# Rotary embedding on one core: the first batch of x loaded as even partitions, then odd partitions

## The chip, the core and the metric

The kernel runs on one core of a Trainium2 chip. The metric is the time of one execution on the device, in microseconds (us); the median of three runs is used.

## What is computed

```
x:   (16, 512, 1024) float32       # batch, sequence, 16 heads of 64
cos, sin: (512, 32) float32        # one row of 32 for each sequence position
x1, x2 = x[..., :32], x[..., 32:]  # halves of each head
out = concatenate([x1*cos - x2*sin, x1*sin + x2*cos], axis=-1)   # (16, 512, 16, 64) float32
```

Everything stays in float32. x is 33.55 MB and the output is as large, so 67.1 MB have to cross between device memory and the core's on-chip memory.

## The kernel before, in words

**Tiles.** Batches 0, 1, 14 and 15 are tiles of their own ("singles"), the other twelve batches form six pairs: ten tiles, t = 0 to 9. A single puts four sequence positions on each of the 128 partitions, which is one contiguous run of 16 KB of device memory for each partition; a pair puts eight positions on each partition, 32 KB. One sequence position on all 128 partitions is a "row" of 128x1024 numbers (0.5 MB); there are 64 rows, u = 0 to 63. `x_sb` is a ring of 40 rows in on-chip memory, and results are written over the x that they come from.

**Loads.** All are issued by ScalarE's queue (ACTq), in the order of the tiles. The first six tiles (40 rows, 20 MB) fill the ring and are issued at once. After tile 0 the two tables cos and sin (64 KB each) are issued on the same queue (L174), then the other five loads. The remaining four loads wait until the stores that empty their place in the ring have landed (L194).

**Work on a row.** VectorE (DVE) multiplies x by cos into PSUM (`mul`, L293). GpSimd (POOL) multiplies the swapped halves of x by the signed sin table into `t2_sb` (L257); six of the 64 rows have this done by VectorE instead (L286). Then the two are added: for 43 rows by VectorE (`comb`, L304), for 21 rows by TensorE, which adds `t2_sb` into PSUM by a product with the identity (L224), after which ScalarE copies the sum to `x_sb` (L191). GpSimd takes the rows strictly in order.

**Stores.** SyncE's queue (SPq, L161) issues one store for each tile as soon as the last row of the tile is added.

**Start.** A load's completion adds 16 to the tile's semaphore `sem_in[t]`. GpSimd waits at the first row of a tile for that semaphore (L255), and before tile 0 also for the signed sin table, which ScalarE makes from `stage` (L182, L183); VectorE waits for the cos table first (L263), copies it to PSUM (L264), and then waits for the tile's semaphore (L279). TensorE and ScalarE make the tables for the pairs from the same `stage` (L208, L186, L187).

Of the kernel before, what the change touches and what calls it, by code (L numbers as in the profile page):

```python
# [6 lines left out]
def bass_split_heads_rope_kernel(  # L7
# [20 lines left out]
    P = 128  # L28
# [35 lines left out]
    EH = H * HD // BANK  # L64
    LEAD = 1
    LAG = 10

    with ExitStack() as stack:
        x_sb = stack.enter_context(nc.sbuf_tensor([P, RING, H, 2, HALF], fp32))
# [10 lines left out]
        sem_in = [stack.enter_context(nc.semaphore(f"in{t}")) for t in range(NT)]  # L80
# [20 lines left out]
        def c_of(t, r):  # L101
            return c1_ps[:, r, :] if tiles[t][1] == R1 else pair_ps[:, r // R1, 0, r % R1, :]

        def s_of(t, r):
            return s1_sb[:, r] if tiles[t][1] == R1 else s2_sb[:, r]

        x1 = x.rearrange("b (s r) d -> b s (r d)", r=R1)
        o1 = out.rearrange("b (s r) h d -> b s (r h d)", r=R1)
        x2 = x.rearrange("b (s r) d -> s b (r d)", r=R2)
# [3 lines left out]
        def in_dram(single, pairs, t):  # L113
            b, n = tiles[t]
            return single[b] if n == R1 else pairs[:, b:b + 2, :]

        def in_sbuf(t):
            b, n = tiles[t]
            k = b * R1 % RING
            return x_sb[:, k:k + n].rearrange("p n h t d -> p (n h t d)")  # L120

        def where(u):
            t, r = rows[u]
            return t, r, u % RING

        def swapped(k):
            return x_sb[:, k, :, ::-1, :]

        def over_heads(table):
            return table[:, None, :, :].broadcast_to([P, H, 2, HALF])  # L130
# [8 lines left out]
        def wait_t2_free(eng, u):  # L139

            if u >= NT2:
                v = u - NT2
                if PE2[v]:
                    eng.wait_ge(sem_e, n_pe[v])
                else:
                    eng.wait_ge(sem_v, n_comb[v])
# [3 lines left out]
            return sum(b * R1 // R2 == k for b, _ in tiles)  # L150

        def load(eng, t):
            eng.dma_start(in_sbuf(t), in_dram(x1, x2, t)).then_inc(sem_in[t], 16)  # L153

        def on_sync(sp):
            for u in range(NU):
# [7 lines left out]
        def on_scalar(ae):  # L164
            later = {}
            for t, (b, n) in enumerate(tiles):
                if b * R1 + n <= RING:
                    load(ae, t)
                else:

                    later.setdefault((b * R1 - RING) // R2 * R2 + R2 - 1 + LAG, []).append(t)
                if t == 0:
                    for i, (table, sem) in enumerate(((cos, sem_cos), (sin, sem_sin))):
                        ae.dma_start(stage[:, i, :], table.rearrange("(s r) d -> s (r d)", r=R1)).then_inc(sem, 16)  # L174
# [13 lines left out]
            for u in range(NU):  # L188
                if PE2[u]:
                    ae.wait_ge(sem_e, n_pe[u])  # L190
                    ae.activation(xs[:, u % RING, :], t1_ps[:, u % NT1, :], COPY).then_inc(sem_a, 1)  # L191
                for t in later.get(u, ()):
                    k = (tiles[t][0] * R1 - RING) // R2
                    ae.wait_ge(sem_out[k], 16 * stores_of(k))  # L194
                    load(ae, t)
# [38 lines left out]
        def on_gpsimd(pl):  # L234
            pl.memset(ident[:], 1.0).then_inc(sem_i, 1)  # L235
            pl.wait_ge(sem_i, 1)
            pl.affine_select(  # L237
                out=ident[:],
                in_=ident[:],
                compare_op=mybir.AluOpType.is_equal,  # L240
                fill=0.0,
                base=0,
                pattern=[[-1, P]],
                channel_multiplier=1,
            ).then_inc(sem_i, 1)
            for u in range(NU):
                if V2[u]:
                    continue
                t, r, k = where(u)
                if (t, r) == (0, 0):  # L250
                    pl.wait_ge(sem_s, 1)
                if (t, r) == (2, 0):
                    pl.wait_ge(sem_s, 2)
                if r == 0:
                    pl.wait_ge(sem_in[t], 16)  # L255
                wait_t2_free(pl, u)
                pl.tensor_tensor(  # L257
                    t2_sb[:, u % NT2, :, :, :], swapped(k), over_heads(s_of(t, r)), mult
                ).then_inc(sem_p, 1)

        def on_vector(ve):
            ve.memset(zero[:], 0.0).then_inc(sem_z, 1)  # L262
            ve.wait_ge(sem_cos, 16)  # L263
            ve.tensor_copy(c1_ps, stage[:, 0, :].rearrange("s (r d) -> s r d", d=HALF)).then_inc(sem_c, 1)  # L264
            ve.wait_ge(sem_c, 1)
            ve.wait_ge(sem_w, NT1 * EH)

            def pair_tables():
                ve.wait_ge(sem_s, 2)
                row = pair_ps[:, V_ROW // R1, 1, V_ROW % R1, :]  # L270
                ve.tensor_scalar_mul(v_ps[:, 0, :], row, -1.0).then_inc(sem_c, 1)
                ve.tensor_copy(v_ps[:, 1, :], row).then_inc(sem_c, 1)

            first_v = V2.index(True)

            def mul(u):
                t, r, k = where(u)
                if r == 0:
                    ve.wait_ge(sem_in[t], 16)  # L279
                if (t, r) == (2, 0):  # L280
                    pair_tables()
                if u == first_v:
                    ve.wait_ge(sem_c, 3)
                if V2[u]:
                    wait_t2_free(ve, u)
                    ve.tensor_tensor(t2_sb[:, u % NT2, :, :, :], swapped(k), over_heads(v_ps), mult)  # L286
                if u >= NT1:
                    v = u - NT1
                    if PE2[v]:
                        ve.wait_ge(sem_a, n_pe[v])  # L290
                    else:
                        ve.wait_ge(sem_v, n_comb[v])
                ve.tensor_tensor(  # L293
                    t1_ps[:, u % NT1, :].rearrange("p (h d) -> p h d", d=HALF),
                    x_sb[:, k, :, :, :].rearrange("p h t d -> p (h t) d"),
                    c_of(t, r)[:, None, :].broadcast_to([P, 2 * H, HALF]),
                    mult,
                ).then_inc(sem_m, 1)

            def comb(u):  # L300
                t, r, k = where(u)
                ve.wait_ge(sem_m, u + 1)
                ve.wait_ge(sem_p, n_pool[u])  # L303
                ve.tensor_tensor(  # L304
                    xs[:, k, :],
                    t1_ps[:, u % NT1, :],
                    t2_sb[:, u % NT2, :, :, :].rearrange("p h t d -> p (h t d)"),
                    add,
                ).then_inc(sem_v, 1)

            for u in range(NU + LEAD):
                if u < NU:
                    mul(u)
                if u >= LEAD and not PE2[u - LEAD]:
                    comb(u - LEAD)

        on_sync(nc.sync)
        on_scalar(nc.scalar)
        on_gpsimd(nc.gpsimd)
        on_tensor(nc.tensor)  # L320
        on_vector(nc.vector)
# [33 lines left out]
```

## Time and profile before

| | |
|---|---|
| Median of three runs | 161.4 us (161.15 to 161.4) |
| The profiled execution, first to last instruction (its span) | 160.3 us; no time of its own is listed beside it |
| Bytes moved | 67.26 MB, 419 GB/s over the span |
| Share of the span in which an engine is busy | GpSimd 84%, VectorE 81%, TensorE 45%, ScalarE 15% |
| DMA: share of 16 engines' span | loads' queue 49.6%, stores' queue 48.9% |
| Loads: time from issue to landing | 8.0 us shortest, 67.5 us longest |

The page cuts the span into 40 slices of 4.0 us and gives for each the busy share of every engine in tenths. A "landing" is the moment at which a transfer's semaphore has its full count. The time from issue to landing contains the time that a transfer spends behind others in its queue. DMA shares over 1 occur in short stretches because a packet's time is counted by its recorded start and end.

### The profile page before, as it was taken

The page shows a single profiled execution, that of the slowest core. Times are in us where ns is not written, and L with a number is a line of the kernel's source. Part 1 is how long each engine was busy: PE and PEld are TensorE (multiplying, and loading weights), DVE is VectorE, ACT ScalarE, POOL GpSimd, SP SyncE. Part 2 cuts the span into 40 slices and gives each one's busy share as a digit, 9 for nine tenths or more (in the row PEclk, how much of TensorE's full clock was granted, in tenths as well). Part 3 has the DMA queues.
Part 4 walks back from the last instruction along what each step waited for, and adds up shares of the span by engine and source line. Part 5 has one row for each costly group of instructions (what it writes and reads, how often), then busy time and mean ns, then how long its engine had stood idle before and what let it go on. Part 6 is the DMA issues. An engine that isn't in the chain of part 4 may idle for free.

```text
span 160.3 us, 522 instructions
## 1 busy us (share of the span) xinstructions
PE 72.8 (45%) x94; PEld 24.0 (15%) x94; DVE 130.3 (81%) x117; ACT 24.4 (15%) x27; POOL 134.9 (84%) x64
## 2 busy tenths in 40 slices
PE   6050004478357936660847105489458435850000
PEld 1020002022202211210221002022202111220000
DVE  0069998599989999996999709899889999999500
ACT  0420000203120222022012010201220402040000
POOL 1059999999999999999999999699999999289400
PEclk9955555557755587689687965555555977699555
DMA  5999999999999999999999999999999999999896
GB/s 147 409 441 474 409 450 409 425 429 429 446 429 458 417 411 466 409 433 401 450 433 425 425 409 458 409 433 433 411 429 462 441 417 401 450 441 441 376 450 294
DMA packets 3170, 67.26 MB, mean 419 GB/s; under 512 B 352, under 2 KB 608, under 8 KB 608
## 3 DMA queue, kind: packets, MB, share of 16 engines
q10 hardware_dynamic: 1728, 33.69, 49.6%
q1 hardware_dynamic: 1440, 33.56, 48.9%
q14 instruction: 2, 0.02, 0.0%
HBM read 33.69 MB, written 33.55 MB: 419 GB/s over the span
## 4 chain that ended last, share of the span: by engine, by line
DMA 60%; POOL 13%; DVE 8%; PE 7%; issue 3%; ACT 2%; ACTq 1%; DVEq 0%
DMA x_sb<-in_x_dram 41%; DMA out_dram<-x_sb 18%; POOL t_sb L257 13%; PE t_ps L224 7%; DVE t_ps L293 5%; DVE x_sb L304 3%; ACT x_sb L191 2%; ACTq L153 1%; ACTq L174 1%; DVE t_sb L286 0%; DVEq L303 0%
## 5 line engine op out<-in xcount | busy, mean ns | idle before, releaser
L257 POOL TENSOR_TENSOR t_sb<-x_sb,s_sb 128x1024 f32<-128x1024 f32 x58 | 134.2, 2346 | 14.8 <-ACT s_sb L183 8.5
L224 PE MATMUL t_ps<-t_sb,ident 128*128 128x512 f32 x84 | 68.0, 957 | 63.0 <-DVE t_ps L293 39.2
L293 DVE TENSOR_TENSOR t_ps<-x_sb,pair_ps 128x1024 f32<-128x1024 f32 x48 | 57.7, 1223 | 9.9 <-ACT x_sb L191 9.8
L304 DVE TENSOR_TENSOR x_sb<-t_ps,t_sb 128x1024 f32<-128x1024 f32 x43 | 52.4, 1218 | 2.6 <-POOL t_sb L257 2.6
L224 PEld LDWEIGHTS t_ps<-t_sb,ident 128*128 128x128 f32 x84 | 22.1, 290 | 108.9 <-DVE t_ps L293 74.6
L191 ACT ACTIVATE x_sb<-t_ps 128x1024 f32<-128x1024 f32 x21 | 21.5, 1023 | 109.9 <-PE t_ps L224 96.9
L293 DVE TENSOR_TENSOR t_ps<-x_sb,tab_ps 128x1024 f32<-128x1024 f32 x16 | 19.3, 1222 | 0.1
L286 DVE TENSOR_TENSOR t_sb<-x_sb,tab_ps 128x1024 f32<-128x1024 f32 x6 | 7.3, 1213 | 0.0
L264 DVE COPY tab_ps<-stage 128x128 f32<-128x128 f32 x1 | 0.3, 294 | 7.8 <-DMA stage<-in_cos_dram 7.8
L208 PE MATMUL pair_ps<-stage,pick 128*128 128x256 f32 x4 | 2.0, 667 | 5.4 <-DMA stage<-in_sin_dram 5.4
L201 PE MATMUL t_ps<-zero 128*128 128x512 bf16 x6 | 2.7, 627 | 1.3 <-DVE zero L262 1.3
L208 PEld LDWEIGHTS pair_ps<-stage,pick 128*128 128x128 f32 x4 | 1.2, 324 | 6.4 <-issue 6.3
L177 ACT ACT_TABLE_LOAD x1 | 1.3, 1283 | 5.5 <-issue 5.5
L201 PEld LDWEIGHTS t_ps<-zero 128*128 128x128 bf16 x6 | 0.7, 136 | 2.4 <-DVE zero L262 1.2
L262 DVE MEMSET zero<- 128x256 uint32 x1 | 0.3, 272 | 0.9 <-PEq L337 0.9
L186 ACT ACTIVATE s_sb<-pair_ps 128x256 f32<-128x256 f32 x1 | 0.4, 383 | 1.7 <-PE pair_ps L208 1.7
L182 ACT ACTIVATE s_sb<-stage 128x128 f32<-128x128 f32 x1 | 0.3, 309 | 2.1 <-DMA stage<-in_sin_dram 2.1
L235 POOL MEMSET ident<- 128x128 f32 x1 | 0.2, 204 | 0.3 <-POOLq L337 0.3
L177 ACT ACTIVATE pick<-ident 128x256 f32<-128x256 f32 x1 | 0.4, 416 | 0.0
L187 ACT ACTIVATE s_sb<-pair_ps 128x256 f32<-128x256 f32 x1 | 0.4, 379 | 0.0
L237 POOL TENSOR_SCALAR_AFFINE_SELECT ident<-ident 128x128 f32<-128x128 f32 x1 | 0.3, 292 | 0.1
L337 POOL MEMSET const-float32-0.0<- 128x1 f32 x1 | 0.1, 98 | 0.3 <-issue 0.3
(6 smaller groups left out, 1.0 us busy)
## 6 DMA issues: line engine op xcount, KB each, us to landing
x_sb<-in_x_dram ACTq DMA_DIRECT2D x6, 4096.0 KB, 38.0
out_dram<-x_sb SPq DMA_DIRECT2D x6, 4096.0 KB, 25.0
x_sb<-in_x_dram ACTq DMA_DIRECT2D x4, 2048.0 KB, 22.6
out_dram<-x_sb SPq DMA_DIRECT2D x4, 2048.0 KB, 15.2
stage<-in_cos_dram ACTq DMA_DIRECT2D x1, 64.0 KB, 7.8
stage<-in_sin_dram ACTq DMA_DIRECT2D x1, 64.0 KB, 7.5
```

The lines of the kernel that those rows point to most:

```text
L153: eng.dma_start(in_sbuf(t), in_dram(x1, x2, t)).then_inc(sem_in[t], 16)
L174: ae.dma_start(stage[:, i, :], table.rearrange("(s r) d -> s (r d)", r=R1)).then_inc(sem, 16)
L177: ae.activation(pick[:], ident[:].rearrange("q (s k) -> q k s", k=2)[:, :, :, None].broadcast_to([P, 2, P // 2, 2]), COPY).then_inc(sem_g, 1)
L186: ae.activation(s2[:, :, :, 0, :], pair_ps[:, :, 1, :, :], COPY, scale=-1.0)
L191: ae.activation(xs[:, u % RING, :], t1_ps[:, u % NT1, :], COPY).then_inc(sem_a, 1)
L201: pe.matmul(t1_ps[:, k, b * BANK:(b + 1) * BANK], zero[:, 0:P], zero[:], start=True, stop=True).then_inc(sem_w, 1)
L208: pe.matmul(pair_ps[:, k].rearrange("p c r d -> p (c r d)"), pick[:, k].rearrange("q s b -> q (s b)"), stage[:].rearrange("q c f -> q (c f)"),
L224: ins = pe.matmul(t1_ps[:, u % NT1, b * BANK:(b + 1) * BANK], ident[:], t2[:, b * BANK:(b + 1) * BANK], start=False, stop=True, skip_group ...
L257: pl.tensor_tensor(t2_sb[:, u % NT2, :, :, :], swapped(k), over_heads(s_of(t, r)), mult).then_inc(sem_p, 1)
L286: ve.tensor_tensor(t2_sb[:, u % NT2, :, :, :], swapped(k), over_heads(v_ps), mult)
L293: ve.tensor_tensor(t1_ps[:, u % NT1, :].rearrange("p (h d) -> p h d", d=HALF), x_sb[:, k, :, :, :].rearrange("p h t d -> p (h t) d"), c_of ...
L304: ve.tensor_tensor(xs[:, k, :], t1_ps[:, u % NT1, :], t2_sb[:, u % NT2, :, :, :].rearrange("p h t d -> p (h t d)"), add,).then_inc(sem_v, 1)
```

## The change

The load of tile 0 is issued as two transfers, in place of one: first the partitions 0, 2, 4, ..., 126 and then 1, 3, 5, ..., 127, each partition with the same 16 KB as before. Each of the two adds 16 to `sem_in[0]`, so the two waits for tile 0 (on GpSimd and on VectorE) wait for 32. Nothing starts work on one half alone. The tables and all other loads follow behind the two on the same queue, unchanged.

```
+    FIRST = 2
...
         def load(eng, t):
-            eng.dma_start(in_sbuf(t), in_dram(x1, x2, t)).then_inc(sem_in[t], 16)
+            if t:
+                eng.dma_start(in_sbuf(t), in_dram(x1, x2, t)).then_inc(sem_in[t], 16)
+                return
+            for i in range(FIRST):
+                eng.dma_start(in_sbuf(t)[i:P:FIRST], in_dram(x1, x2, t)[i:P:FIRST]).then_inc(sem_in[t], 16)
...
                 if r == 0:
-                    pl.wait_ge(sem_in[t], 16)
+                    pl.wait_ge(sem_in[t], 16 * (FIRST if t == 0 else 1))
...
                 if r == 0:
-                    ve.wait_ge(sem_in[t], 16)
+                    ve.wait_ge(sem_in[t], 16 * (FIRST if t == 0 else 1))
```

## The prediction

> **What bounds the kernel now.** I read the page first, for the shares and the slices.
>
> ```profile
> DMA  5999999999999999999999999999999999999896
> GB/s 147 409 441 474 409 450 409 425 429 429 446 429 458 417 411 466 409 433 401 450 433 425 425 409 458 409 433 433 411 429 462 441 417 401 450 441 441 376 450 294
> q10 hardware_dynamic: 1728, 33.69, 49.6%
> q1 hardware_dynamic: 1440, 33.56, 48.9%
> ```
>
> Only the first slice and the last few are below 9 tenths, and between the first slice and the last the rate stays at 376 to 474 GB/s whether loads run alone (slices 2 to 5), with stores, or stores alone near the end. A rate that doesn't depend on the direction or the mix looks like a ceiling of the 16 DMA engines or of their way into on-chip memory. So DMA time lost anywhere before the last load is lost to the whole stream of loads. The chain that ended last says the same:
>
> ```profile
> 2.87 18.56 DMA x_sb<-in_x_dram
> ...
> 93.45 47.51 DMA x_sb<-in_x_dram
> 140.96 0.07 issue
> 141.02 9.29 POOL t_sb L257 x4
> ...
> 150.40 1.23 DVE x_sb L304
> ```
>
> The last load is issued at 93.4 and lands at 140.96, 47.5 us later, because it stands behind other loads and shares the engines with stores. Behind it come four rows on GpSimd (9.3 us), one addition (1.2) and the last store (issued at 151.7, 8.6 us to the end at 160.3): a tail of 19.3 us that the change doesn't touch. GpSimd's timeline shows the slack ahead of that tail:
>
> ```profile
> 9.85 90.09 POOL L257 TENSOR_TENSOR t_sb<-x_sb,s_sb 128x1024 f32<-128x1024 f32 x39 [8.48 <-ACT s_sb L183]
> 101.72 9.29 POOL L257 TENSOR_TENSOR t_sb<-x_sb,s_sb 128x1024 f32<-128x1024 f32 x4 [1.78 <-PE t_ps L224]
> ...
> 141.02 9.27 POOL L257 TENSOR_TENSOR t_sb<-x_sb,s_sb 128x1024 f32<-128x1024 f32 x4 [3.92 <-DMA x_sb<-in_x_dram]
> ```
>
> The brackets give the idle time before each piece and what ended it. GpSimd is 3.92 us early for the last tile: a late start of the arithmetic alone, with the loads as they are, can be swallowed there; lost DMA time can't.
>
> The start, from the timeline and from the table of short stretches (last three columns: granted clock, DMA share, GB/s):
>
> ```profile
> 0.81 0.37 ACTq L153 DMA_DIRECT2D x_sb<-in_x_dram  x1
> 1.21 0.46 ACTq L174 DMA_DIRECT2D stage<-in_cos_dram  x1
> 1.69 0.45 ACTq L174 DMA_DIRECT2D stage<-in_sin_dram  x1
> ...
> 9.04 0.29 DVE L264 COPY tab_ps<-stage 128x128 f32<-128x128 f32 x1 [7.84 <-DMA stage<-in_cos_dram]
> ```
>
> ```profile
> 1.00:2.00 1.00, 0.75 (x2) 0.28 (x3) 0.19 (x1) 0.00 (x0) 0.29 (x1) 1.00 0.54 98
> 2.00:3.00 1.00, 1.00 (x4) 0.36 (x3) 0.00 (x0) 0.00 (x0) 0.00 (x0) 1.00 0.75 180
> 3.00:4.00 1.00, 0.99 (x3) 0.08 (x1) 0.00 (x0) 0.00 (x0) 0.00 (x0) 1.00 0.83 311
> 4.00:5.00 1.00, 0.00 (x0) 0.00 (x0) 0.00 (x0) 0.00 (x0) 0.00 (x0) 1.00 1.00 426
> ```
>
> Tile 0 is issued at 0.81 and lands 8.0 us later (the shortest time to landing of any load), at 8.8; cos at 9.0, sin at 9.2 (7.8 and 7.5 us after their issue). VectorE waits for cos, GpSimd for sin, which stands last in that queue. The rate climbs for three microseconds: 98 + 180 + 311 GB/s makes 0.59 MB by 4.0.
>
> **The change part by part.** *One more issue on ACTq.* One issue takes 0.37 to 0.46 us with 0.03 between, so cos, sin and the five loads behind them are issued about 0.4 us later. The engines need the tables only when tile 0 is through, near 7.5 (0.59 MB by 4.0, the other 1.51 MB at 426 GB/s: 3.5 us). cos and sin issued at 1.6 and 2.1 are there by then; ScalarE's own first work has 2.08 us of idle time before sin. Cost nothing; without that cover it would be 0.4.
>
> *Sixteen more completion packets.* The loads' queue has 1728 packets for twelve transfers, which is 12 x (128 + 16): one per partition and one per engine for completion. Now it has 1744. The queue's share, 49.6% of 16 x 160.3 us over 1728 packets, is 0.74 us a packet, and those are 19.5 KB on average; a completion packet carries almost nothing. At worst one per engine costs 0.74 us, at best nothing. I take nothing, as the tables' small packets are the nearest: cos and sin, 288 packets together, put only 0.4 us between the landing of tile 0 and that of sin.
>
> *A second landing.* Both waits are now for the second half's landing. Three transfers in one queue land within 0.4 us here, so waiting for completion isn't paid one after the other: cost 0. [...]
>
> *The rate of a transfer to every second partition.* This is the term that decides, and no row here shows one: every transfer in the trace covers 128 partitions. [...] Bounds: at best the half runs at the 426 GB/s of the row at 4.0, cost 0, or the slow climb before 4.0 gets shorter: at 426 from 2.0 on, 0.85 MB would have come in place of 0.49, a gain of at most 0.36 MB / 426 GB/s = 0.85 us. At worst it stays at the lowest rate of a full microsecond with the queue already filled, 180 GB/s: 1.51 MB / 180 in place of 1.51 / 426, 8.4 - 3.5 = +4.9 us. I take half the steady rate, 213 GB/s, that is, that the partitions of one half bring two engines at a time onto one way into on-chip memory. That lies nearer to the 180 row than to the 426 row, and I choose it because the steady rate looks like a ceiling of such ways: it is alike for both directions. 1.51 / 213 = 7.1 in place of 3.5, **+3.5 us**; the climb, which is below or near 213 anyway, is left as it is.
>
> [...]
>
> *Where the loss goes.* The landing of tile 0, the tables, and every later load move by 3.5 us; GpSimd starts at 13.4 in place of 9.85, and everything it paces, the stores included, moves along. Nothing absorbs it: the 3.92 us stay, since the load they wait for is late by as much. Sum: span 160.3 + 3.5 = 163.8. The median of the runs is 1.1 above the span; 161.4 + 3.5 = **164.9 us**.
>
> **The rivals.** *No change.* The halves run at 426 GB/s; the queue hides the rest, 161.4 within 0.3. For it: all partitions get the same bytes in packets of the same 16 KB, and the queue is never empty. Against it: the steady ceiling says that which way an engine uses matters, and the new shape alters that.
>
> *Faster.* Smaller transfers let all engines begin sooner or spread the first reads better, and the climb gains half of its 0.85 us: 161.0. For it: the shares of 0.54, 0.75 and 0.83 before 4.0 show engines without work, or slow, while the queue has it. Against: the first issue comes at the same 0.81. It decides from about 0.7 MB moved by 4.0.
>
> *Slower by latency.* The second half's completion comes 1 to 2 us late though the engines lose nothing, and the slack isn't there when needed (at 101.72 GpSimd waits 1.78 for TensorE, at 141.02 3.92 for the load): up to 162.5. It needs a slip beyond the slack.
>
> **How the numbers follow.** A measurement of this kernel can tell about 0.2% (0.3 us) from no change. Half rate: 0.56, all slower, between 163 and 166.3 (+1.6 for a partial loss, +4.9). No change: 0.22, of which 0.11 within 0.2%, 0.05 below and 0.06 above. Faster start: 0.17. Latency: 0.05. Faster 0.05 + 0.17 = 0.22; same 0.11; slower 0.56 + 0.06 + 0.05 = 0.67. The cases have both signs. The likeliest one's own range is 163.0 to 166.3; the range that is to hold 8 in 10 has to reach to no change and to most of the faster start: 160.9 to 166.3, which leaves out gains over 0.5 us and the odd case above.
>
> **What would show it.** Right: in the stretches from 4.0 to 8.0 the GB/s fall to about 210 to 260 in place of 344 to 442; the cos wait of VectorE ends near 12.5 in place of 9.04; GpSimd's first multiplication starts near 13.4; the second and third slices together carry some 1.5 MB less; the wait at the last tile is still near 3.9 and the tail 19.3. Wrong: 400 GB/s or more from 4.0 on and cos within 0.3 us of 9.0 (no change); or more than 0.7 MB by 4.0 and an earlier cos (faster start). If tile 0 lands late and the end doesn't move, the chain from the first load to the last is what I have misread.

## The result, and the profile after

The changed kernel takes 161.94 us (median of 21 runs) against 161.32 us before (21 runs beside them): a ratio of 1.0037, 95% interval 1.0027 to 1.0046, that is 0.6 us slower (0.4 to 0.7). Ratios and intervals, here and below, are taken from the executions that were not in a slower state of the chip. The forecast was 164.9, 3.5 us slower. The sign was right; the size was wrong by a factor of six.

The page of the changed kernel comes first: the slices, the rates and the loads' queue.

```profile
span 160.2 us, 523 instructions
...
DMA  4999999999999999999999999999999999999896
GB/s 147 391 444 491 393 393 401 450 421 491 397 393 458 419 491 401 401 507 401 393 507 409 393 491 417 401 442 413 440 421 479 405 417 434 454 417 474 356 454 286
...
q10 hardware_dynamic: 1744, 33.69, 49.6%
```

The 16 more packets are there (1744), and the forecast hole in the second and third slices is not: 391 and 444 GB/s, against 409 and 441 before. The span is even 0.1 us shorter than on the page before. That comparison misleads. The span that the runs list for each execution is 1.4 us below its time, in every kernel of this study; the page before has 160.3, but the executions of the same kernel beside the experiments have median spans of 159.8 to 159.9, and the changed kernel's is 160.5. So the page before shows an execution about 0.5 us longer than usual, the page after one of the shortest of its kernel, and a change of 0.6 us can't be read off two pages.

The start of the changed kernel, from its timeline and from the table of short stretches:

```profile
0.81 1.20 ACTq L159 DMA_DIRECT2D x_sb<-in_x_dram  x2
...
2.05 0.60 ACTq L180 DMA_DIRECT2D stage<-in_cos_dram  x1
...
8.86 0.29 DVE L270 COPY tab_ps<-stage 128x128 f32<-128x128 f32 x1 [7.67 <-DMA stage<-in_cos_dram]
```

```profile
1.00:2.00 1.00, 0.75 (x2) 0.28 (x3) 0.20 (x1) 0.00 (x0) 0.29 (x2) 1.00 0.00 0
2.00:3.00 1.00, 1.00 (x4) 0.37 (x3) 0.00 (x0) 0.00 (x0) 0.00 (x0) 1.00 1.09 262
3.00:4.00 1.00, 0.99 (x3) 0.09 (x1) 0.00 (x0) 0.00 (x0) 0.00 (x0) 1.00 0.84 328
4.00:5.00 1.00, 0.00 (x0) 0.00 (x0) 0.00 (x0) 0.00 (x0) 0.00 (x0) 1.00 0.89 377
```

Two things differ from before. The first issue takes 0.56 us where it took 0.37 (the chain lists 0.56 and 0.61 for the two), and no packet starts between 1.0 and 2.0: the trace's first packet of x starts at 2.18 in place of 1.82. These stretches count a packet, with all its bytes and its whole time, where it starts; that is also why shares over 1 occur. So the 0.59 MB (262 + 328) by 4.0, the same as before, are packets begun; of those of x, 0.33 MB had ended by then on either page. From 4.0 to 8.0 the halves run at 391 GB/s, against 406 in the kernel before:

```profile
4.00:8.00 4.00, 0.00 (x0) 0.00 (x0) 0.00 (x0) 1.28 (x1) 0.00 (x0) 1.00 0.94 391
```

```profile
4.00:8.00 4.00, 0.00 (x0) 0.00 (x0) 0.00 (x0) 1.70 (x2) 0.00 (x0) 0.96 0.97 406
```

The first line is of the changed kernel, the second of the kernel before. The tail is as before: the last tile's wait and the four rows after it on GpSimd,

```profile
140.89 9.27 POOL L263 TENSOR_TENSOR t_sb<-x_sb,s_sb 128x1024 f32<-128x1024 f32 x4 [3.83 <-DMA x_sb<-in_x_dram]
```

and 19.3 us from there to the end. Two kernels that turned out as fast as the one before ("second" and "gap" below) have pages with spans of 159.7 and 159.8, the same 19.3 us at the end, and this line at 140.37 and 140.52. So what the change costs arises ahead of the landing of the last load.

### The profile page after: what moved, and what is told of

Same layout as the page of the kernel before. It is cut to its first block, busy times and chain, and to the rows that moved or that the text cites. A ratio compares the mean times of both kernels' runs of the same rounds, so it can differ in the third digit from the quotient of the medians.

```text
span 160.2 us, 523 instructions
## 1 busy us (share of the span) xinstructions
PE 71.3 (44%) x94; PEld 23.8 (15%) x94; DVE 130.4 (81%) x117; ACT 24.4 (15%) x27; POOL 134.8 (84%) x64
## 3 DMA queue, kind: packets, MB, share of 16 engines
q10 hardware_dynamic: 1744, 33.69, 49.6%
## 4 chain that ended last, share of the span: by engine, by line
DMA 59%; POOL 13%; DVE 8%; PE 7%; issue 4%; ACTq 2%; ACT 2%; DVEq 0%
DMA x_sb<-in_x_dram 40%; DMA out_dram<-x_sb 18%; POOL t_sb L263 13%; PE t_ps L230 7%; DVE t_ps L299 5%; DVE x_sb L310 3%; ACT x_sb L197 2%; ACTq L180 1%; ACTq L159 1%; ACTq L156 1%; DVE t_sb L292 0%; DVEq L309 0%
## 5 line engine op out<-in xcount | busy, mean ns | idle before, releaser
L230 PE MATMUL t_ps<-t_sb,ident 128*128 128x512 f32 x84 | 66.5, 937 | 64.3 <-DVE t_ps L299 40.3
L299 DVE TENSOR_TENSOR t_ps<-x_sb,tab_ps 128x1024 f32<-128x1024 f32 x16 | 19.3, 1222 | 0.1
```

Source lines behind the costliest of these rows:

```text
L230: ins = pe.matmul(t1_ps[:, u % NT1, b * BANK:(b + 1) * BANK], ident[:], t2[:, b * BANK:(b + 1) * BANK], start=False, stop=True, skip_group ...
L299: ve.tensor_tensor(t1_ps[:, u % NT1, :].rearrange("p (h d) -> p h d", d=HALF), x_sb[:, k, :, :, :].rearrange("p h t d -> p (h t) d"), c_of ...
```

## The experiments

Each ratio is to the kernel before, timed on the same chip in the same rounds; a loss in us is the ratio less 1, times 161.3. The runs weigh four theories: the prediction's (a transfer to half the partitions runs at half the rate); the first descriptor (a transfer of 64 partitions starts later); something in the second transfer itself; an instruction more, outside the span.

**halves: neighbouring partitions.**

```
-                eng.dma_start(in_sbuf(t)[i:P:FIRST], in_dram(x1, x2, t)[i:P:FIRST]).then_inc(sem_in[t], 16)
+                eng.dma_start(in_sbuf(t)[i * P // FIRST:(i + 1) * P // FIRST], in_dram(x1, x2, t)[i * P // FIRST:(i + 1) * P // FIRST]).then_inc(sem_in[t], 16)
```

> Tile 0 in two transfers as after the change, but partitions 0 to 63 and then 64 to 127. Theory of the first descriptor (a transfer of 64 rows starts its first packets about 0.36 us later, near 2.18 in place of 1.82, and the whole stream of loads is late by some tenths): the same late start and 161.8 to 162.1 us. Theory of the prediction (the partitions of a transfer share ways into on-chip memory, which every second partition happened to escape): neighbouring halves run at half rate, VectorE's wait for cos ends near 12 and the time is 164 to 165. Theory of the instruction outside the span (one more DMA costs a few tenths between the span and the measured time): 161.8 to 162.0, with time minus span near 1.45 us.

Measured: 1.0302 (1.0264 to 1.0341), 4.9 us slower (4.3 to 5.5), above the 164 to 165 us that were expected. Two stretches of 4 us of this kernel (last column GB/s), then its first row on GpSimd:

```profile
4.00:8.00 4.00, 0.00 (x0) 0.00 (x0) 0.00 (x0) 1.70 (x2) 0.00 (x0) 1.00 0.94 197
8.00:12.00 4.00, 0.00 (x0) 0.00 (x0) 0.00 (x0) 0.00 (x0) 0.00 (x0) 1.00 0.97 199
```

```profile
14.43 90.10 POOL L263 TENSOR_TENSOR t_sb<-x_sb,s_sb 128x1024 f32<-128x1024 f32 x39 [13.06 <-ACT s_sb L189]
```

From 4.0 to 8.0 the engines are as busy as in the changed kernel (0.94), yet they move half: 197 GB/s against 391. In the trace a packet of 16 KB that starts in that stretch takes 1.16 to 1.29 us here; in the changed kernel all but a few take 0.61 to 0.64. So a half-rate transfer exists and costs what the prediction reckoned and more; but neighbours have it, not alternate partitions. This settles the main miss. It doesn't say what the neighbours share: they are neighbours in device memory too, where each half is one contiguous 1 MB in place of every second 16 KB, and no run changes one side alone.

**four: four transfers of every fourth partition.**

```
-    FIRST = 2
+    FIRST = 4
```

> Tile 0 in four transfers of every fourth partition. If each further transfer costs (an issue of about 0.6 us each on ScalarE's queue, a bubble at each completion packet): three times the loss of the change, 162.9 to 163.3 us. If only the later first packet costs: 161.8 to 162.1 again, first packets near 2.2. If the instruction outside the span costs: three times 0.35 us between span and time, 162.4 to 162.6 with an unchanged span.

Measured: 1.0102 (1.0056 to 1.0148), 1.6 us slower, with a wide scatter between runs. The interval, 0.9 to 2.4 us, lies above what a late first packet alone would cost (it starts at 2.20; "delay" below prices that) and holds three times the change, 1.9 us; so this run leaves a cost per transfer possible. Time less span stays at 1.4, so nothing is lost outside the span. The stretch from 4.0 to 8.0 has 344 GB/s; its 84 packets of 16 KB take 0.75 us in the mean (busy share 0.99), 25 of them over 0.7 and up to 1.85 us. Why those are slow I didn't find out.

**second: tile 1 split like this, tile 0 whole.**

```
-            if t:
+            if t != 1:
...
-pl.wait_ge(sem_in[t], 16 * (FIRST if t == 0 else 1))
+pl.wait_ge(sem_in[t], 16 * (FIRST if t == 1 else 1))     # and the same on VectorE
```

> Tile 0 whole again, tile 1 in two transfers of every second partition: the same number of instructions and packets as after the change, but the extra one stands behind others in the queue. Theory of the first descriptor: the first packets start at 1.82 again and the time is that of before, 161.2 to 161.5 us. Theory of a bubble at a completion packet or of an extra instruction outside the span: the time of after, 161.8 to 162.1.

Measured: 0.9997 (0.9982 to 1.0011), no difference (at most 0.2 us). Its timeline:

```profile
0.81 0.37 ACTq L156 DMA_DIRECT2D x_sb<-in_x_dram  x1
...
2.18 1.30 ACTq L159 DMA_DIRECT2D x_sb<-in_x_dram  x2
```

The first issue takes 0.37 again and the first packet starts at 1.83. The very same two transfers, with their packets, completions and doubled wait, cost nothing that can be measured when they stand behind others. A cost per completion or per instruction wherever it stands is refuted; the loss belongs to the head of the queue.

**actop: one more instruction, no DMA.**

```
+            ae.activation(spare[:, 0:1], ident[:, 0:1], COPY)
             ae.wait_ge(sem_sin, 16)
```

> The kernel before with one more small copy on ScalarE (128x1), in the idle time before the sin table, and no further DMA. Theory of the first descriptor and theory of a bubble: 161.2 to 161.5 us, as before. Theory that any further instruction costs outside the span: 161.6 to 161.9 with time minus span over 1.3 us.

Measured: 1.0007 (0.9988 to 1.0025), time less span 1.4 again. The interval alone reaches a loss of 0.4 us; it is the unchanged 1.4, here and in the changed kernel, that refutes the theory outside the span.

**delay: tile 0 whole, issued later.**

```
             later = {}
+            ae.wait_ge(sem_z, 1)
```

> The kernel before, tile 0 in one transfer, but ScalarE's queue first waits for VectorE's memset (over at about 1.2 us), so the first issue stands at about 1.23 in place of 0.81. It shows what a late first issue by itself is worth. Theory of the first descriptor: the first packets start at about 2.24, as after the change, and the end moves by as much, 0.4 us: 161.6 to 161.8. Theory that the two transfers cost something in themselves at the head of an empty queue, the late start being hidden in the 3.6 to 3.9 us of slack ahead of the last tile: 161.2 to 161.4.

Measured: 1.0016 (1.0005 to 1.0027), 0.26 us slower (0.08 to 0.44). Its first issue and its last tile:

```profile
1.23 0.37 ACTq L153 DMA_DIRECT2D x_sb<-in_x_dram  x1
...
140.82 9.28 POOL L258 TENSOR_TENSOR t_sb<-x_sb,s_sb 128x1024 f32<-128x1024 f32 x4 [3.59 <-DMA x_sb<-in_x_dram]
```

The first packet starts at 2.25, 0.43 later than before. A late first packet costs, and the wait for the last tile is still 3.6, as in "second" and "gap" (3.58 and 3.62): that slack doesn't swallow it, since the load it waits for is late as well, as far as single pages tell (140.82 here, 140.37 and 140.52 there). By the middle value it accounts for less than half of the change's 0.6; the interval allows anything from 0.1 to 0.4 us of it.

**cols: two transfers of tile 0, all partitions, half of the columns each.**

```
+    W = R1 * dim // FIRST
...
-                eng.dma_start(in_sbuf(t)[i:P:FIRST], in_dram(x1, x2, t)[i:P:FIRST]).then_inc(sem_in[t], 16)
+                eng.dma_start(in_sbuf(t)[:, i * W:(i + 1) * W], in_dram(x1, x2, t)[:, i * W:(i + 1) * W]).then_inc(sem_in[t], 16)
```

> Tile 0 in two transfers that each cover all 128 partitions, with half of every row (8 KB). Theory that a transfer to 64 partitions is issued more slowly: the first issue takes 0.37 again, the first packets start at 1.82 and the time is 161.2 to 161.5 us. Theory that a second issue or a second completion at the head costs: 161.8 to 162.1 as after the change. Theory of packets of half the size: a little above before, within 0.3 us, with 256 packets more in the table of queues than packets of completion.

Measured: 1.0024 (1.0013 to 1.0036), 0.4 us slower (0.2 to 0.6). Its short stretches:

```profile
1.00:2.00 1.00, 0.75 (x2) 0.28 (x3) 0.20 (x1) 0.00 (x0) 0.30 (x2) 1.00 0.35 57
2.00:3.00 1.00, 1.00 (x4) 0.36 (x3) 0.00 (x0) 0.00 (x0) 0.00 (x0) 1.00 0.70 197
3.00:4.00 1.00, 1.00 (x3) 0.09 (x1) 0.00 (x0) 0.00 (x0) 0.00 (x0) 1.00 0.98 377
```

The issues are short again (0.38 and 0.46), the first packet starts at 1.84, and by 4.0 this kernel has begun 0.63 MB, more than before. So the late start does belong to transfers of 64 partitions; yet this kernel loses time without it. Its loss lies between the theories and is not decided: it can come from tile 0 in two transfers, or from its 8 KB packets, for which up to 0.3 us was expected and which the change doesn't have.

**second_halves: tile 1 in neighbouring halves.**

```
-            if t:
+            if t != 1:
...
-                eng.dma_start(in_sbuf(t)[i:P:FIRST], in_dram(x1, x2, t)[i:P:FIRST]).then_inc(sem_in[t], 16)
+                eng.dma_start(in_sbuf(t)[i * P // FIRST:(i + 1) * P // FIRST], in_dram(x1, x2, t)[i * P // FIRST:(i + 1) * P // FIRST]).then_inc(sem_in[t], 16)
...                                                                    # and the waits as in "second"
```

> Tile 1, not tile 0, in two transfers of partitions 0 to 63 and 64 to 127. Theory that neighbouring halves lose their time by half rate wherever they stand in the queue: the loss of the neighbouring halves of tile 0 (4.7 us) less what belongs to the late first packet (0.4 to 0.7), 165.2 to 165.7 us. Theory that half rate costs only while nothing else is in the queue (other transfers behind it fill the gaps): 161.3 to 162.5.

Measured: 1.0389 (1.0373 to 1.0404), 6.3 us slower. The slices of its page show the hole, third and fourth:

```profile
GB/s 166 419 208 233 371 402 410 418 438 442 442 426 454 434 444 394 473 402 465 410 458 426 394 473 410 465 402 467 406 454 418 418 454 414 458 418 402 422 264 316
```

208 and 233 GB/s with 16.8 MB (four pairs) queued behind: the work behind doesn't fill the gaps. Here as in "halves" half rate goes with the shape, not with the start. Both expectations were too low; why this place costs some 1.4 us more than the head is not explained.

**two_queues: the odd partitions issued by SyncE.**

```
-            for i in range(FIRST):
-                eng.dma_start(...)
+            for i, q in enumerate((eng, nc.sync)):
+                q.dma_start(...)
...
+        on_scalar(nc.scalar)                 # so that SyncE's load stands ahead of its stores
         on_sync(nc.sync)
-        on_scalar(nc.scalar)
```

> The two transfers of the change, the even partitions issued by ScalarE's queue and the odd ones by SyncE's queue at about the same time. Theory of the first descriptor: a 64-partition transfer still stands first on both queues, first packets near 2.2, 161.7 to 162.1 us. Theory that it is the second issue, 0.6 us, in front of the tables and the later loads that costs: 161.2 to 161.5.

Measured: 1.0036 (1.0024 to 1.0049), 0.6 us, the same as the change. Each queue issues one:

```profile
0.80 0.58 SPq L159 DMA_DIRECT2D x_sb<-in_x_dram  x1
0.81 0.57 ACTq L159 DMA_DIRECT2D x_sb<-in_x_dram  x1
```

Both take 0.57 to 0.58, and the first packet starts at 2.17. cos is issued at 1.41, only 0.2 later than before, and the whole loss is still there: the second issue in front of the tables isn't what costs, and two issues side by side are no remedy.

**gap: tile 0 whole at 0.81, everything behind it issued later.**

```
                 if t == 0:
+                    ae.wait_ge(sem_w, 2)
```

> The kernel before, tile 0 in one transfer at 0.81, but ScalarE's queue waits after it until TensorE's second product is done (about 2.3 us), so the tables and the later loads are issued about 1.0 us later, as they are behind the second transfer of the change (there 0.84 later). Theory that the place which the second issue takes in the queue is the other part of the cost: 161.6 to 161.8. Theory that the engines still have tile 0 to move until 7.5 and nothing behind it is late: 161.2 to 161.4, and the other part lies in the two transfers themselves.

Measured: 1.0002 (0.9993 to 1.0011), nothing. cos was issued at 2.32 in place of 1.21:

```profile
0.81 0.37 ACTq L153 DMA_DIRECT2D x_sb<-in_x_dram  x1
2.32 0.33 ACTq L175 DMA_DIRECT2D stage<-in_cos_dram  x1
```

The place that the second issue takes on ScalarE's queue is free (at most 0.2 us), as the prediction had it.

**delay_gap: both waits.**

```
             later = {}
+            ae.wait_ge(sem_z, 1)
...
                 if t == 0:
+                    ae.wait_ge(sem_w, 2)
```

> Both waits: tile 0 in one transfer is issued at 1.23 in place of 0.81 and the tables at about 2.3, so all issue times are near those of the change, without its split. Theory that the change costs through issue times alone: 161.8 to 162.0, as after the change. Theory that only the late first packet counts among them: 161.5 to 161.7, as with the first wait alone.

Measured: 161.77 us against 161.29 beside it, 0.5 us by the medians; but the ratio of 1.0009 has an interval, 0.9978 to 1.0039, that includes no loss. Two runs of the kernel before, at 163.27 and 163.56, lie about 2 us above the others in these rounds, while all twelve of this one lie from 161.56 to 161.94. This is inconclusive between the two theories: it doesn't exclude that issue times alone, without the split, make up most of the change's loss.

**tabs_whole and tabs_split: the tables ahead of tile 0, which is whole or split.**

```
-                if b*R1 + n <= RING: load(ae, t)
                 if t == 0:
                     for i, (table, sem) in ...: ae.dma_start(stage[:, i, :], ...)
+                if b*R1 + n <= RING: load(ae, t)
```

> The kernel before with the two tables issued ahead of tile 0, not behind it. It is the base for the next run. The tables' packets take less than a microsecond, tile 0 is issued near 1.7 and its first packets start near 2.7: late by 0.9, which by the rate of the first wait (0.26 us for 0.42) gives 161.6 to 162.0 us.

> The same with tile 0 in the two transfers of the change, so that a transfer of 64 partitions no longer stands first in the queue. Theory that the change costs as the first transfer of an empty queue, and by its slower issue: the engines wait for x at this place too, so a loss of 0.2 to 0.4 us against the run with the tables ahead of the whole tile. Theory that only the very first transfer of the program starts slowly: within 0.2 us of that run. Theory that the second transfer costs at the head in any case: 0.4 to 0.6 us above it.

Measured: 1.0052 (1.0042 to 1.0063) and 1.0066 (1.0057 to 1.0074). "tabs_split" is the same edit, made to the changed kernel. With the tables first, tile 0's first packets start at 2.82 when it is whole and at 3.03 when it is split, and the times are 162.05 and 162.34 us. So the slower start of a 64-partition transfer isn't the program's first issue alone: here it is 0.2 us, and the end is 0.3 us later. That is what the first theory expected, and less than the 0.4 to 0.6 of the theory that the second transfer costs at the head in any case, though the two intervals overlap. Both kernels are slower than before: x should stand first.

**extra, cols_delay, after_again.** The first adds a small transfer between tile 0 and the tables; the second puts the wait of "delay" ahead of "cols"; the third is the changed kernel again.

```
                 if t == 0:
+                    ae.dma_start(spare[:], cos...).then_inc(sem_x, 16)      # extra
...
             later = {}
+            ae.wait_ge(sem_z, 1)                                          # cols_delay, on top of cols
```

> The kernel before, tile 0 in one transfer, with one more small transfer (the cos table a second time, 64 KB, into memory that nothing reads) between tile 0 and the tables. Theory that a second transfer at the head of the queue costs 0.35 us by itself: 161.6 to 161.8. Theory that it has to be a second part of tile 0: its 64 KB at 426 GB/s, 0.15 us, so 161.3 to 161.5.

> Tile 0 in two transfers of half the columns and all 128 partitions, the first of them issued at 1.23 in place of 0.81 by the wait for VectorE's memset. Theory that the late first packet (0.26 us for 0.42) and the second transfer of tile 0 (0.37 us) are two costs that add up to the change: 161.8 to 162.05. Theory that they share one cause: 161.6 to 161.75.

> The changed kernel once more, on the chip and beside the runs of the other two, so that they are compared on equal terms: 161.8 to 162.1 us by both theories.

Measured: 1.0014 (1.0002 to 1.0027), 1.0053 (1.0033 to 1.0074) and 1.0049 (1.0025 to 1.0073). The extra transfer costs 0.2 us (0.0 to 0.4): the middle is near the 0.15 of its own bytes, but the interval holds the 0.35 of the other theory as well, so this run doesn't decide. The late start and the column split together cost 0.5 to 1.2 us, with 0.85 in the middle; their separate losses make 0.26 + 0.39 = 0.65, and the change beside them lost 0.4 to 1.2. So these two add up, and one cause for both (161.6 to 161.75 expected, 162.05 measured) does not fit. The sum also fits the change within what these runs can tell, which doesn't show that the change consists of the same two.

## Why the prediction was right or wrong

**The step that failed** is the rate of a transfer to every second partition. I took half the steady rate, 213 GB/s and +3.5 us, for a shape that no row showed, by arguing that alternate partitions bring two engines onto one way into on-chip memory. That was an assumption: no run shows such a way, nor 213 GB/s for this shape. The runs show that a half rate exists, at 197 to 199 GB/s, for partitions 0 to 63 and 64 to 127, and that alternate partitions escape it: 391 GB/s from 4.0 to 8.0, against 406 before. By the prediction's own sum, an estimate, 1.51 MB at 391 in place of 406 make 0.1 us in place of 3.5. For neighbouring halves the price would have been too low rather than too high: 4.9 us against 3.5. What the argument lacked was the question which partitions go into one transfer. Whether the neighbours share something on the side of on-chip memory or of device memory, no run here shows.

**The rival "no change"** had the rate right and came nearest, but its time of 161.4 within 0.3 misses the measured median by 0.2. The rival "faster" asked for 0.7 MB by 4.0; it was 0.59, as before. What stood against it held: the first issue came at the same 0.81, and it even took longer. The rival "slower by latency" had a mechanism that the runs don't show: no completion came 1 to 2 us late, a figure that no row had given (VectorE's wait for cos ended at 8.86; in "second" and "gap" it was 8.65 and 8.90), and the doubled wait cost nothing in "second".

**The further issue at nothing**: right for the place that it takes in the queue, by "gap"; that an issue would take 0.37 to 0.46 us was wrong for 64 partitions (0.56 and 0.61). **The completion packets and the second landing at nothing**: right where the two transfers stand behind others, by "second"; at the head no run prices them alone. **The slack of 3.9 us ahead of the last tile**: I said that a late start of the arithmetic alone could be swallowed and lost DMA time could not. "delay" agrees with the second half, and it is why a late first packet is seen at the end at all. **The 1.1 us between span and median**: the median time lies 1.4 above the median span; the page before shows a longer execution than most. The sum stands on the median, so nothing came of it.

**What was missing from the sum** is a late start. A transfer of 64 partitions takes 0.56 us to issue in place of 0.37, and its first packet starts 0.36 us later; a wait that makes the first packet 0.43 later costs 0.26 us (0.08 to 0.44). By the middle values that leaves about 0.35 us of the 0.6 to something else.

**What stays open** is that rest. It is not the place of the second issue in the queue ("gap", "two_queues") and not the two transfers wherever they stand ("second"). A second cost of tile 0 in two transfers is the likeliest reading: "cols" loses 0.4 us (0.2 to 0.6) without any late start, and "cols_delay" shows that such a loss and a late start add up. But it isn't shown, since "cols" also doubles the packets, at half the size. Against it, splitting tile 0 behind the tables cost only 0.3 us with a start 0.2 later, and "delay_gap", which has late issues and no split, lost 0.5 us by the medians. Nor does "extra" exclude that any second transfer at the head costs. On the page of "cols" the last load lands at 140.7 though more bytes had been begun by 4.0 than before; single pages scatter by as much as the rest itself, so they can't say where it goes. What was not run is the change's own two transfers at the head without the late start.

**The range**, 160.9 to 166.3, holds the measured time because it reached to "no change", not because the forecast was near. That the sign was right is luck: the loss that was foreseen isn't there, and the one that is there was priced at nothing.

No run of this study beat the kernel before beyond its interval; the whole tile in one transfer, issued first, remains the best start.

## What to carry to other kernels

When a transfer is cut by partitions, ask which partitions go into one transfer before pricing it: here alternate partitions kept 391 GB/s and neighbours fell to 197, in the same number of transfers and bytes. The same cut by alternate partitions cost nothing measurable (at most 0.2 us) behind a filled queue and 0.6 us at the head of an empty one, so look at where in the queue an edit stands before counting its instructions. And before comparing two pages, compare their spans with the spans of the other executions: the page of the slower kernel here was the shorter one.

## What the runs showed of the hardware that was not expected

- Issuing a transfer of 64 partitions as the first took 0.55 to 0.58 us (the change, "halves", "two_queues"), on ScalarE's and on SyncE's queue, against 0.37 to 0.38 for one of 128 partitions; the first packet started at 2.16 to 2.23 against 1.82 to 1.84, where the issue stood at 0.8.
- Transfers to 64 neighbouring partitions keep the engines as busy (share 0.94) at half the rate (197 GB/s, against 391 for alternate ones): here the busy share of DMA alone did not tell the bytes moved.
- A hole of half rate cost more with tile 1, with 16.8 MB queued behind it (6.3 us), than with tile 0 at the head (4.9 us, its late start included).
